# Two transformer blocks on one core: values of the dilated attention in token order, a merged projection block, another pace for the modulation, and expert weights in 8 KB tiles

## Chip, cores and metric

The kernel runs on one core of a Trainium2 chip. The metric is the device time of one execution in microseconds (us). A core has a tensor engine for products (PE, with its loads of the stationary operand, PEld), a vector engine (DVE), a scalar engine (ACT), GpSimd (POOL) and a sync engine (SP) that issues most of the transfers, in order.

## What is computed

A first block of two layers (gated linear attention, short convolution, neighbourhood attention, a convolutional FFN; 512 tokens, and a context of 256 in layer 0), then a second block with four branches over the same 512 tokens (A dilated window attention, B sparse attention with an index, C a time mix, D a state-space mixer), and a mixture of 32 experts, two per token. The parts that the change touches, cut from the reference:

```python
mod = jax.nn.silu(c) @ w_ada[layer] + b_ada[layer]                 # modulation: 6 vectors of 1024
u = modulate(rmsnorm(x, norm_mix_g[layer]), sh1, sc1) @ w_in[layer]
...
A_PATTERNS = ((128, 1), (512, 4), (2048, 16))                      # window, dilation
for q, kp, vp, (win, dil) in zip(qs, kps, vps, A_PATTERNS):
    qb = ...reshape(b, nq, dil, A_HEADS, HEAD_DIM)                 # tokens by residue class
    s = jnp.einsum('barhe,bcrhe->brhac', qb, kb).astype(jnp.float32) * scale
    ...
    o = jnp.einsum('brhac,bcrhe->barhe', p, vb)
...
expert = g_sel * EXPERTS_PER_GROUP + e_sel                         # 2 of 32 experts for each token
return grouped_expert_ffn(x2d, expert, gate, w_gate, w_up, w_down) # silu(x Wg) * (x Wu) @ Wd
```

## The kernel before

Activations lie transposed, channels on partitions and tokens along the rows. Most products keep float32 accuracy by splitting both operands into a high part (`whi`, `hi`; cast on ACT, L287) and a low part (`wlo`, `lo`; difference on DVE, L289): three products, high by high, low by high, high by low, make one (L829 in the first block, L191 to L195 and L1222 to L1224 in the second). Raw weights come by SP (L276) into a few tiles of `k.wpool`. A planner (`Weave.run`) interleaves generator streams: each `yield` names an engine and an estimated cost, and the planner issues the step that can start first; so the order on each engine is fixed when the program is built.

*First block.* `layer` makes one block of 128 output channels after another: `blk` loads a block of `w_in_t`, and `dense` does eight rounds of three products on 512 latent and, where wanted, 256 context columns. Heads 4 and 5 of the gated linear attention are 64 channels in k and in q; each of the two blocks GK45 and GQ45 holds its 64 channels twice, so that both partition halves have them. Between blocks `more(n)` works off n pieces of a queue, `k.adaq` (L255 to L260): "H" pieces load 512 KB of `w_adaH` and take four products on DVE, "B" turns a finished vector round, "P" and "F" are pieces for PE. n is `ada_n`, 0.6 in layer 0 and 0.4 in layer 1. A norm that needs a modulation vector makes all pieces that are still missing (`need`).

*Second block.* `second` lists the streams. `dense2` makes one block of 128 channels of a branch, `values2` the values with tokens on partitions: for each of 4 chunks of 128 tokens and 8 of 128 channels, three products whose stationary operand is the token slice of x (`x2h`, `x2l`) and whose moving operand is 256 columns of weights. `StageA.values` (L1833) does this for the three dilations; group 0 takes adjacent tokens (`nat`), groups 1 and 2 every fourth token (`res`), since `StageA.attend` works on one residue class r at a time. `stage_vb` does the same for branch B (`k.vb`). Results of this size lie in the pool `t1`, 16 tiles of 1 KB per partition: 4 hold `vb` until the last B attend, 12 the three groups' values, and masks and probabilities use what is left. `t2` has 34 tiles of 2 KB. `StageB.index` finds the 256 largest scores by 16 rounds on DVE.

*Experts.* `experts` computes 33 blocks of 64 token rows: experts 0 to 22 in order, a second block for a busy expert at place 23 (after place 22), then the others; `expert_block` takes 16 products for gate and up and 8 for down. Weights of an expert are six parts of 1 MB. Experts with even numbers are loaded into 24 `t2` tiles by 24 transfers of 256 KB (2 KB of each partition's row, L2328), those with odd numbers into six `ew` tiles by transfers of 1 MB (8 KB rows, L2323); there are seven `ew` tiles, in the pool `ep`, which lies over the space of weights, x2 and the branch weights. At the start of block p the loads of expert p + 2 are issued. Each block's output goes to DRAM (`yd`). `gates` computes the gate values on DVE ahead of block 0. `beyond` is a loop for further blocks; it does not run on these inputs (33 output copies for 33 blocks).

Of the kernel before, what the change touches and what calls it, by code (L numbers as in the profile page):

```python
# [239 lines left out]
def ada_prep(k):  # L240

    nc = k.nc
    cc = k.cpool.tile([128, 8, 2], FT, name="cc", tag="cc")
    nc.sync.dma_start(cc, k.ap["c2"])
    k.cs = k.cpool.tile([128, 8, 32], FT, name="cs", tag="cs")
    nc.gpsimd.memset(k.cs, 0.0)
    k.act(k.cs[:, :, 0:2], cc, AF.Silu)
    k.ada_due = 0
    k.mods, k.bada, k.g = {}, {}, {}
    tiles = lambda *qs: [4 * q + i for i in range(4) for q in qs]  # L250

# [586 lines left out]
GLR, GK0, GQ0, GK45, GQ45, NAK, NAQ, GR, SCC, SCH, SCB = 0, 1, 2, 3, 4, 5, 8, 11, 14, 16, 18  # L838


def layer(k, w, l, x, xt, src):
# [116 lines left out]
    ada_n = 0.6 if upd else 0.4  # L958
# [250 lines left out]
def values2(k, name, j, kcs, n, view, store):  # L1209
# [21 lines left out]
nat = lambda x, t: x[:, t * 128:(t + 1) * 128]  # L1231
res = lambda x, t: x[:, t::4]
# [351 lines left out]
def stage_vb(k):  # L1584
# [8 lines left out]
    yield from values2(k, "w2_vb", None, (4, 4), 264, nat, store)  # L1593
# [233 lines left out]
class StageA:  # L1827
# [489 lines left out]
def load_expert(k, src, small):  # L2317

    out = [None] * 24
    for j in (0, 2, 1, 3, 4, 5):  # L2320
        w = None if small else k.ep.tile([128, 2048], FT, tag="ew", name="ew", bufs=k.NEW)
# [7 lines left out]
    return out  # L2329


def rows(k, blks, blk):
# [4 lines left out]
    oh = [t1(k, [128, 4 // n, n, 64]) for _ in range(n)]  # L2337
# [10 lines left out]
    def part(i, after=None):  # L2348
# [9 lines left out]
        out.append(t1(k, [128, 2, 64 * n]))  # L2358
# [5 lines left out]
def expert_block(k, x, W, ydst, queue, fill=()):  # L2364
# [15 lines left out]
    HT = t1(k, [128, 4, 64])  # L2380
# [14 lines left out]
def experts(k, W, routing):  # L2395
# [24 lines left out]
    gates(k)  # L2420
    for i, b in enumerate(order):
        p = b if b < 32 else SWAP
        if 0 < p < 30 and b < 32:
            W.append(load(p + 2))
        if b == 31:
            n = nc.values_load(k.eid[0:1, 16:17], min_val=0, max_val=15)
        if b == 30:
            ln2 = [[t2(k) for _ in range(2)] for _ in range(2)]
            for a in range(2):
                for h in range(2):  # L2430
                    nc.sync.dma_start(ln2[a][h], k.ap["ln2"][a][:, h * 512:(h + 1) * 512])
# [9 lines left out]
def beyond(k, n):  # L2441

    tc, nc = k.tc, k.nc
    with tc.For_i(0, n, 1) as i:  # L2444
# [5 lines left out]

        def weights(n):
            t = k.ep.tile([128, 512], FT, tag="bw", name="bw", bufs=4)
            nc.sync.dma_start(t, k.ap["w_exp"][bass.ds(e, 1), n // 4].rearrange("a p n -> (a p) n")[:, n % 4 * 512:n % 4 * 512 + 512])
            return t
# [7 lines left out]
def gates(k):  # L2462
# [5 lines left out]
    for t in range(4):  # L2468
        d = t1(k, [128, 2, 128])
# [5 lines left out]
def finish(k, ln2, out):  # L2475
# [9 lines left out]
    for t in range(4):  # L2485
        y = k.ep.tile([128, 2048], FT, tag="ew", name="ew", bufs=k.NEW)
# [130 lines left out]
def body(tc, ap):  # L2617
    nc = tc.nc
    with ExitStack() as st:
# [4 lines left out]
        k.csd = k.dp.tile([2, 128, 1024], FT, name="csd", tag="csd")  # L2624
        k.yd = k.dp.tile([NB * 64, 1024], FT, name="yd", tag="yd")
# [3 lines left out]
        with ExitStack() as sw:  # L2629
            k.wpool = sw.enter_context(tc.tile_pool(name="w", bufs=1, side="right"))  # L2630
            with ExitStack() as s1:
# [25 lines left out]
                k.hp = sw.enter_context(tc.tile_pool(name="h2", bufs=1, side="right"))  # L2657
# [12 lines left out]
        next(routing)  # L2670
        finish(k, experts(k, W, routing), ap["out"])
# [6 lines left out]
def hostprep(I):  # L2678
# [17 lines left out]
    cols=[w[:,:,768:800],z, w[:,:,192:320], w[:,:,0:128], w[:,:,320:384],w[:,:,320:384], w[:,:,128:192],w[:,:,128:192], w[:,:,2336:2720], w[:,:,1952:2336], w[:,:,800:1184], w[:,:,1440:1696], w[:,:,1696:1952], w[:,:,1184:1440]]  # L2696
# [133 lines left out]
```

## Time and profile before

| | us |
|---|---|
| median of three executions | 3198.53 (3196.09 to 3203.12) |
| the profiled execution | 3198.1 |
| its span | 3196.2 |
| PE busy | 3003.7 (94%) |
| PE's stationary loads busy | 2275.4 (71%) |
| DVE busy | 1531.5 (48%) |
| ACT busy | 989.5 (31%) |
| POOL busy | 565.8 (18%) |

The first block runs to about 1830, the second to about 2648, the experts to 3163, then the sum of two outputs per token and the last norm. The rows below come from one profiled execution. In a timeline a row is one instruction, or xN alike ones in a row, with its start and length; PE's matmuls overlap, so what a matmul costs is the distance between starts and not its length. "PEld" is the load of the stationary operand. In the table of stretches the granted clock is a share of PE's full clock, and the DMA share is the mean busy share of the core's 16 DMA engines. A row of waits names the engine, tile and line that waited, and what ended the wait.

### The profile page before, as it was taken

How to read it: one execution, taken by the hardware profiler on the slowest of the kernel's cores; microseconds unless marked ns; L12 is line 12 of the kernel's file. 1: busy time of each engine (PE TensorE's matmuls, PEld its weight loads, DVE VectorE, ACT ScalarE, POOL GpSimd, SP SyncE). 2: the span in 40 equal slices, each digit the busy share in tenths (PEclk: the TensorE clock that was granted, in tenths of full speed). 3: DMA queues.
4: the chain of work that ended last, by engine and by line, in shares of the span. 5: the costliest groups of instructions: out<-in, count | busy, mean ns of one | idle time of the engine just before them, and what ended most of it. 6: DMA issues, size and time to landing. Idle time of an engine off the chain costs nothing. (4 is left out here: it accounts for less than half of the span.)

```text
span 3196.2 us, 42551 instructions
## 1 busy us (share of the span) xinstructions
PE 3003.7 (94%) x16248; PEld 2275.4 (71%) x16248; DVE 1531.5 (48%) x3049; ACT 989.5 (31%) x1649; POOL 565.8 (18%) x569
## 2 busy tenths in 40 slices
PE   7999997999999899989999999999998989999998
PEld 5878676888887687767777778878776765544453
DVE  3566857644536626744443456525545562111112
ACT  4243314322323324343332443233242521111111
POOL 2331301210102123131121131220001010000002
PEclk9999998999999899999999999999998999999999
DMA  6411333322324431232222330042131359999997
GB/s 232 142 57 49 120 107 98 107 85 86 109 83 148 132 94 58 69 99 79 90 93 89 96 109 21 14 142 73 55 106 47 98 196 352 393 378 389 391 396 290
DMA packets 159838, 461.29 MB, mean 144 GB/s; under 512 B 20912, under 2 KB 28752, under 8 KB 147344
## 3 DMA queue, kind: packets, MB, share of 16 engines
q1 hardware_dynamic: 145296, 434.05, 38.7%
q0 software_dynamic: 7776, 19.70, 1.8%
q10 hardware_dynamic: 6560, 4.79, 0.5%
q8 instruction: 130, 2.13, 0.3%
q14 instruction: 76, 0.62, 0.1%
HBM read 435.40 MB, written 19.92 MB: 142 GB/s over the span
## 5 line engine op out<-in xcount | busy, mean ns | idle before, releaser
L289 DVE TENSOR_TENSOR wlo<-wraw,whi 128x1024 fp32r<-128x1024 f32 (+2 forms) x276 | 339.4, 1231 | 444.9 <-ACT whi L287 427.9
L287 ACT CAST whi<-wraw 128x1024 fp32r<-128x1024 f32 (+2 forms) x276 | 285.6, 1036 | 793.6 <-PE at L829 287.7
L829 PE MATMUL mm<-hi,whi 128*128 128x512 f32 (+1 forms) x1152 | 476.1, 416 | 33.1 <-ACT hi L448 13.8
L829 PE MATMUL mm<-lo,whi 128*128 128x512 f32 (+1 forms) x1152 | 462.2, 401 | 11.9 <-DVE lo L451 10.8
L829 PE MATMUL mm<-hi,wlo 128*128 128x512 f32 (+1 forms) x1152 | 458.9, 400 | 14.6 <-DVE wlo L289 14.5
L829 PEld LDWEIGHTS mm<-hi,whi 128*128 128x128 f32 (+1 forms) x1152 | 217.1, 189 | 106.7 <-issue 32.9
L829 PEld LDWEIGHTS mm<-hi,wlo 128*128 128x128 f32 (+1 forms) x1152 | 217.6, 189 | 72.2 <-DVE wlo L289 17.4
L829 PEld LDWEIGHTS mm<-lo,whi 128*128 128x128 f32 (+1 forms) x1152 | 217.6, 189 | 64.0 <-DVE lo L451 12.2
L829 PE MATMUL mm<-b,whi 128*128 128x512 f32 x704 | 242.9, 398 | 7.1 <-ACT whi L287 6.5
L191 PE MATMUL mm<-x2h,whi 128*128 128x512 f32 x512 | 210.9, 413 | 7.3 <-ACT pcx L1251 4.7
L195 PE MATMUL mm<-x2h,wlo 128*128 128x512 f32 x512 | 204.3, 399 | 2.0 <-DVE wlo L289 2.0
L193 PE MATMUL mm<-x2l,whi 128*128 128x512 f32 x512 | 205.1, 401 | 0.1
L1120 POOL TENSOR_TENSOR b<-b,b 128x768 f32<-128x768 f32 (+1 forms) x44 | 71.9, 1635 | 679.4 <-DVE b L797 650.5
L2374 DVE COPY GU<-mm 64x512 f32<-64x512 f32 x33 | 22.9, 694 | 352.8 <-ACT GU L171 352.8
L829 PEld LDWEIGHTS mm<-b,whi 128*128 128x128 f32 x704 | 132.2, 189 | 40.8 <-ACT whi L287 7.8
L2354 PEld LDWEIGHTS gl<-t,gt 128*128 128x128 f32 x1088 | 128.0, 194 | 30.1 <-issue 16.4
L1087 DVE SCALAR_TENSOR_TENSOR b<-mm,mods,b 128x512 f32<-128x512 f32 x64 | 48.0, 750 | 210.3 <-PE mm L829 210.3
L2354 PE MATMUL gl<-t,gt 128*128 128x128 f32 (+1 forms) x1088 | 136.8, 280 | 3.8 <-DVE t L2344 3.8
L829 PE MATMUL mm<-b,wlo 128*128 128x512 f32 x352 | 138.6, 398 | 1.3 <-DVE wlo L289 1.2
L2371 PE MATMUL mm<-ew,t 128*64 128x512 f32 x256 | 117.7, 609 | 16.4 <-DMA ew<-w_exp 16.3
L829 PE MATMUL at<-hi,whi 128*128 128x256 f32 x416 | 118.2, 284 | 2.1 <-ACT hi L448 2.0
L191 PEld LDWEIGHTS mm<-x2h,whi 128*128 128x128 f32 x512 | 97.9, 191 | 31.3 <-ACT pcx L1251 5.1
(570 smaller groups left out, 6488.5 us busy)
## 6 DMA issues: line engine op xcount, KB each, us to landing
t<-w_exp SPq DMA_DIRECT2D x384, 256.0 KB, 5.9
ew<-w_exp SPq DMA_DIRECT2D x96, 1024.0 KB, 12.2
wraw<-ffn_up SPq DMA_DIRECT2D x88, 512.0 KB, 3.3
wraw<-w_t SPq DMA_DIRECT2D x64, 512.0 KB, 3.3
wraw<-w_adaH SPq DMA_DIRECT2D x48, 512.0 KB, 3.3
wraw<-w_in_t SPq DMA_DIRECT2D x40, 512.0 KB, 3.5
wraw<-w_adaF SPq DMA_DIRECT2D x32, 512.0 KB, 3.6
wraw<-ffn_dn SPq DMA_DIRECT2D x32, 448.0 KB, 3.2
```

The source lines that it names most:

```text
L191: nc.tensor.matmul(ps, whi[:, i, :], xs_(xh, kc, ts), start=st, stop=False)
L193: nc.tensor.matmul(ps, whi[:, i, :], xs_(xl, kc, ts), start=False, stop=False)
L195: nc.tensor.matmul(ps, wlo[:, i, :], xs_(xh, kc, ts), start=False, stop=sp)
L287: nc.scalar.copy(hi, raw)
L289: nc.vector.tensor_tensor(lo, raw, hi.bitcast(FT), op=OP.subtract)
L829: nc.tensor.matmul(p, w[:, kc - min(kcs)], x[:, sl], start=a, stop=e)
L1087: nc.vector.scalar_tensor_tensor(x[m][:, sl], p, k.mods[l][:, 8 * q + m, s:s + 1], x[m][:, sl], op0=OP.mult, op1=OP.add)
L1120: nc.gpsimd.tensor_tensor(y0[:, :N], y0[:, :N], y1[:, :N], op=OP.mult)
L2354: mm = nc.tensor.matmul(ps[:, c], k.x1[t][h][:, cs], oh[t * n // 4][:, t % (4 // n)].rearrange("p a b -> p (a b)"), start=(t == 0), stop=( ...
L2371: last = nc.tensor.matmul(gu[64:128], x(kc), W(8 + kc), start=(kc == 0), stop=(kc == 7)).ins
L2374: nc.vector.tensor_copy(GU[64:128], gu[64:128])
```

## The change

- `StageA.values`: groups 1 and 2 also take adjacent tokens. Each chunk's result is written to a DRAM buffer `vd` (128 KB), and four loads with row step 4 bring the residue classes into four new `t1` tiles.
- `layer`: GK45 and GQ45 become one block GKQ (64 channels of k, 64 of q); its evacuation `twice` writes each half to both partition halves by copies. `w_in_t` has 19 blocks per layer instead of 20.
- Modulation: `ada_n` is 1.05 in layer 0 and 0.7 in layer 1; the queue goes vector by vector, with five turns instead of four.
- Experts: all but expert 0 are loaded in parts of 1 MB into 19 tiles of 8 KB rows, `ew` (7) and `ew2` (12). `ew2` is opened after block 0, when the pools of constants `c3` and of `t1`, `t2` (`b2`) are closed; the rest of expert 2 is loaded and the gates are computed then. Rows, gathered inputs and HT are in a new tag `s1` (14 tiles). At the start expert 1's first five parts are loaded, then expert 0, expert 1's last part and expert 2's first.
- Pools: the first block's weight pool `w` closes behind it; the second block has its own, `w2`, beside `h2` on the right side.

The core of the diff (the weights' layout on the host, the output norm's tiles and the loop `beyond` are left out):

```diff
-    a, b, c = tiles(2), tiles(3, 4) + tiles(5), tiles(0, 1)
-    k.adaq += H(0, a, 1, True) + [("B", 0)] + H(0, a, 0, False) + H(0, b, 0, True) + [("B", 1)] + H(0, b, 1, False)
-    k.adaq += H(1, c, 1, True) + [("B", 0)] + H(1, c, 0, False) + [("B", 2)]
+    h = 1
+    for l, js in ((0, tiles(2)), (0, tiles(3, 4)), (0, tiles(5)), (1, tiles(0, 1))):
+        k.adaq += H(l, js, h, True) + [("B", 1 - h)] + H(l, js, 1 - h, False)
+        h = 1 - h
+    k.adaq.append(("B", 2))
...
-GLR, GK0, GQ0, GK45, GQ45, NAK, NAQ, GR, SCC, SCH, SCB = 0, 1, 2, 3, 4, 5, 8, 11, 14, 16, 18
+GLR, GK0, GQ0, GKQ, NAK, NAQ, GR, SCC, SCH, SCB = 0, 1, 2, 3, 4, 7, 10, 13, 15, 17
...
-    ada_n = 0.6 if upd else 0.4
+    ada_n = 1.05 if upd else 0.7
...
+    def twice(ps):
+
+        for d, p, c in ((g.kk, 0, True), (g.q, 64, upd)):
+            t = d[1] = k.b3()
+            yield cA(1.1)
+            for h in (0, 64):
+                nc.scalar.copy(t[h:h + 64, LAT], ps[0][p:p + 64])
+            if c:
+                yield cV(0.6)
+                for h in (0, 64):
+                    nc.vector.tensor_copy(t[h:h + 64, CTX], ps[1][p:p + 64])
+
     tk, tq = [None] * 2, [None] * 2
-    for i in range(2):
-        tk[i] = blk(GK0 + 2 * i, True, to(g.kk, i, True))
-        more(ada_n)
-        tq[i] = blk(GQ0 + 2 * i, upd, to(g.q, i, upd))
-        more(ada_n)
+    tk[0] = blk(GK0, True, to(g.kk, 0, True))
+    more(ada_n)
+    tq[0] = blk(GQ0, upd, to(g.q, 0, upd))
+    more(ada_n)
+    tk[1] = tq[1] = blk(GKQ, True, twice)
+    more(2 * ada_n)
...
-            h, l = view(xh[:, kc], t), view(xl[:, kc], t)
+            h, l = (x[:, kc, t * 128:(t + 1) * 128] for x in (xh, xl))
...
     def values(s, g):
         k, nc = s.k, s.k.nc
         v = s.v[g] = [t1(k) for _ in range(4)]
-        yield from values2(k, "w2_va", g, (4, 4), 256, nat if g == 0 else res, lambda t, ps: nc.scalar.copy(v[t], ps))
+        if g == 0:
+            yield from values2(k, "w2_va", g, (4, 4), 256, lambda t, ps: nc.scalar.copy(v[t], ps))
+            return
+
+
+        def store(t, ps):
+            nc.scalar.copy(v[t], ps)
+            nc.sync.dma_start(k.vd[g - 1, t * 128:(t + 1) * 128], v[t])
+        yield from values2(k, "w2_va", g, (4, 4), 256, store)
+        s.v[g] = [t1(k) for _ in range(4)]
+        yield cN(2.5)
+        for r in range(4):
+            nc.sync.dma_start(s.v[g][r], k.vd[g - 1, r::4])
...
-def load_expert(k, src, small):
-
-    out = [None] * 24
-    for j in (0, 2, 1, 3, 4, 5):
-        w = None if small else k.ep.tile([128, 2048], FT, tag="ew", name="ew", bufs=k.NEW)
+def big(k):
+
+    k.turns = (k.turns + 1) % (k.NEW + k.NEW2) if k.ep2 else (k.turns + 1) % k.NEW
+    if k.turns < k.NEW:
+        return k.ep.tile([128, 2048], FT, tag="ew", name="ew", bufs=k.NEW)
+    return k.ep2.tile([128, 2048], FT, tag="ew2", name="ew2", bufs=k.NEW2)
+
+
+def s1(k, shape):
+    return k.ep.tile(list(shape), FT, tag="s1", name="s1", bufs=k.NS1)
+
+
+def load_parts(k, out, js, src, small=False):
+
+    for j in js:
+        w = None if small else big(k)
         if w:
             k.nc.sync.dma_start(w, src(j, slice(0, 2048)))
         for c in range(4):
@@ -2326,7 +2360,9 @@
             out[4 * j + c] = t2(k) if small else w[:, cs]
             if small:
                 k.nc.sync.dma_start(out[4 * j + c], src(j, cs))
-    return out
+
+
+PARTS = (0, 2, 1, 3, 4, 5)
...
-    oh = [t1(k, [128, 4 // n, n, 64]) for _ in range(n)]
+    oh = [s1(k, [128, 4 // n, n, 64]) for _ in range(n)]
...
     def load(p):
-        small = p % 2 == 0
+        W.append([None] * 24)
         if p < EARLY:
-            return load_expert(k, lambda j, c: k.ap["w_exp"][p, j][:, c], small)
+            load_parts(k, W[p], PARTS, lambda j, c: k.ap["w_exp"][p, j][:, c])
+            return
         e = nc.values_load(k.eid[0:1, 17 + p:18 + p], engines=(mybir.EngineType.SP,), min_val=0, max_val=31)
-        return load_expert(k, lambda j, c: k.ap["w_exp"][bass.ds(e, 1), j].rearrange("a p n -> (a p) n")[:, c], small)
-
-    W.append(load(2))
+        load_parts(k, W[p], PARTS, lambda j, c: k.ap["w_exp"][bass.ds(e, 1), j].rearrange("a p n -> (a p) n")[:, c])
+
     for f in gather(0, k.blk0):
         f()
     drain(routing)
-    gates(k)
...
-            W.append(load(p + 2))
+            load(p + 2)
...
+        if i == 0:
+            sb.close()
+            k.ep2 = k.pool("ep2")
+            load_parts(k, W[2], PARTS[k.NEW - 6:], lambda j, c: k.ap["w_exp"][2, j][:, c])
+            gates(k)
...
+                s0.close()
+                k.hp = right(sw, "h2")
+                k.wpool = right(sw, "w2")
...
-            k.c2, k.gtp, k.b2p = k.pool("c2"), k.pool("gt"), k.pool("b2")
-            k.brp = sw.enter_context(tc.tile_pool(name="br", bufs=1, side="right"))
-            k.NT2, k.NT1, k.NEW = 34, 16, 7
-            consts2(k)
-            acc = [t2(k) for _ in range(8)]
-            second(k, acc)
-            W = [load_expert(k, lambda j, c: ap["w_exp"][0, j][:, c], True)]
-        k.ep = k.pool("ep")
-        W.append(load_expert(k, lambda j, c: ap["w_exp"][1, j][:, c], False))
+        k.c2, k.gtp = k.pool("c2"), k.pool("gt")
+        k.c3, k.b2p = (sb.enter_context(tc.tile_pool(name=n, bufs=1)) for n in ("c3", "b2"))
+        k.brp = right(sw, "br")
+        k.NT2, k.NT1, k.NEW, k.NEW2, k.NS1, k.turns, k.ep2 = 34, 16, 7, 12, 14, -1, None
+        consts2(k)
+        acc = [t2(k) for _ in range(8)]
+        second(k, acc)
+        sw.close()
+        k.ep = right(st, "ep")
+        W = [[None] * 24 for _ in range(3)]
+        for p, js in ((1, PARTS[:5]), (0, PARTS), (1, PARTS[5:]), (2, PARTS[:k.NEW - 6])):
+            load_parts(k, W[p], js, lambda j, c, p=p: ap["w_exp"][p, j][:, c], p == 0)
```

## Rows read from the trace of the kernel before

**Rows 1.** Stretches: us; busy us (count) PE, PEld, DVE, ACT, POOL; clock, DMA share, GB/s.
```profile
2648.40:2810.00 161.60, 161.60 (x927) 82.06 (x928) 31.05 (x113) 20.59 (x44) 10.44 (x20) 1.00 0.99 373
2810.00:2997.00 187.00, 173.31 (x926) 84.74 (x924) 25.72 (x81) 21.11 (x44) 11.37 (x22) 0.98 1.01 387
2997.00:3163.00 166.00, 160.15 (x894) 79.32 (x890) 19.99 (x51) 20.71 (x44) 10.33 (x20) 1.00 0.99 382
```
**Rows 2.** Stretches of the second block's middle (columns as in rows 1).
```profile
2171.00:2220.00 49.00, 47.59 (x208) 40.49 (x207) 25.63 (x45) 15.39 (x32) 2.88 (x2) 1.00 0.17 54
2220.00:2280.00 60.00, 53.97 (x226) 42.28 (x225) 54.22 (x114) 17.56 (x25) 7.73 (x6) 0.94 0.21 71
```
**Rows 3.** Waits of PE, 2655 to 3163.
```profile
PE mm L2371 <- DMA ew<-w_exp: 16.3, 11, 2.1
```
**Rows 4.** Groups by line, stationary loads, 2155 to 2171; busy us, mean ns | idle before.
```profile
L1222 PEld LDWEIGHTS mm<-whi,x2h 128*128 128x128 f32 x32 | 6.1, 189 | 0.3
```
**Rows 5.** Groups by line, stationary loads, 2280 to 2307.
```profile
L1222 PEld LDWEIGHTS mm<-whi,x2h 128*128 128x128 f32 x31 | 10.2, 328 | 0.3 <-issue 0.2
```
**Rows 6.** Timeline of PE at 2159: start us, us, line, operation.
```profile
2158.92 0.28 PE L1224 MATMUL mm<-whi,x2l 128*128 128x256 f32 x1
...
2159.27 0.28 PE L1224 MATMUL mm<-whi,x2l 128*128 128x256 f32 x1
```
**Rows 7.** Timeline of PE at 2297.
```profile
2297.14 0.40 PE L1224 MATMUL mm<-whi,x2l 128*128 128x256 f32 x1
...
2297.84 0.40 PE L1224 MATMUL mm<-whi,x2l 128*128 128x256 f32 x1
```
**Rows 8.** The tile Y: an expert block's output copies and their write-backs.
```profile
L2390 ACT COPY Y<-mc x33: 586/586/587, 2663.4 to 3162.8; 128x512 f32<-128x512 f32 x33
...
DMA to landing us min/median/max: 2.3/4.3/7.3
```
**Rows 9.** Timeline of PE at 373, layer 0's projections.
```profile
373.11 0.40 PE L829 MATMUL mm<-hi,whi 128*128 128x512 f32 x1
...
375.22 0.39 PE L829 MATMUL mm<-hi,whi 128*128 128x512 f32 x1
```
**Rows 10.** Timeline of PE at 1310, layer 1's projections.
```profile
1309.60 0.39 PE L829 MATMUL mm<-hi,whi 128*128 128x512 f32 x1
...
1311.69 0.40 PE L829 MATMUL mm<-hi,whi 128*128 128x512 f32 x1
```
**Rows 11.** Timeline of SP's load queue, 290 to 520 (consecutive issues in one row).
```profile
359.19 24.96 SPq L276 DMA_DIRECT2D wraw<-w_adaH  x8
```
**Rows 12.** Waits of PE, 380 to 510: total us, times, longest us.
```profile
PE mm L829 <- DVE wlo L289: 13.6, 2, 8.4
```
**Rows 13.** Stretches of the expert loads (columns as in rows 1).
```profile
2908.00:2914.00 6.00, 6.00 (x27) 2.02 (x28) 0.42 (x1) 0.59 (x1) 1.03 (x2) 1.00 1.02 427
...
2956.00:2968.00 12.00, 12.00 (x70) 5.88 (x71) 2.46 (x11) 1.33 (x3) 1.03 (x2) 1.00 1.05 388
2834.90:2852.90 18.00, 14.40 (x71) 5.68 (x70) 0.85 (x2) 1.52 (x4) 1.03 (x2) 1.00 1.02 418
2810.00:3120.00 310.00, 296.31 (x1620) 146.41 (x1618) 41.78 (x124) 37.08 (x77) 20.67 (x40) 0.99 1.02 389
```
**Rows 14.** Timeline of SP's load queue, 2570 to 2680.
```profile
2577.47 43.84 SPq L2328 DMA_DIRECT2D t<-w_exp  x24
2622.67 3.61 SPq L2323 DMA_DIRECT2D ew<-w_exp  x6
```
**Rows 15.** Timeline of SP's load queue, 1790 to 1870.
```profile
1805.36 20.19 SPq L276 DMA_DIRECT2D wraw<-w_t  x5
```
**Rows 16.** Timeline of PE, 1821 to 1831.
```profile
1822.50 0.40 PE L829 MATMUL mm<-b,wlo 128*128 128x512 f32 x1
...
1830.34 1.19 PE L191 MATMUL mm<-x2h,whi 128*128 128x512 f32 x2 [0.48 <-ACT x2h L205]
```
**Rows 17.** Timeline of PE, 2440 to 2447, the last attend of the sparse branch.
```profile
2444.12 1.11 PE L1994 MATMUL mc<-t,t 128*64 128x128 f32 x6 [0.46 <-ACT t L1986]
```

More of the change, by code (lines that the diff above doesn't have):

```diff
@@ L1154, in ld @@
 def ld(k, name, shape, dt=FT, key=None):
-    t = k.c2.tile(shape, dt, name=name, tag=name)
+    t = (k.c3 if name in ("tri", "trig", "caus", "pm", "lev", "bd64", "lora") else k.c2).tile(shape, dt, name=name, tag=name)
     k.nc.sync.dma_start(t, k.ap[name])
@@ L1206, in dense2, with values2 @@
     yield "-", "mm", 1
-def values2(k, name, j, kcs, n, view, store):
+def values2(k, name, j, kcs, n, store):
     nc = k.nc
@@ L1228, in values2 @@
     yield "-", "s", 2
-nat = lambda x, t: x[:, t * 128:(t + 1) * 128]
-res = lambda x, t: x[:, t::4]
 class StageC:
@@ L1592, in store @@
         nc.vector.tensor_copy(k.ex[:, t], ps[:, 256:264])
-    yield from values2(k, "w2_vb", None, (4, 4), 264, nat, store)
+    yield from values2(k, "w2_vb", None, (4, 4), 264, store)
 class StageD:
@@ L2357, in part @@
                     k.order(after, mm)
-        out.append(t1(k, [128, 2, 64 * n]))
+        out.append(s1(k, [128, 2, 64 * n]))
         (nc.vector.tensor_copy if i % 2 else nc.scalar.copy)(out[-1], ps)
@@ L2379, in expert_block @@
         last = nc.tensor.transpose(ht[:, i], GU[:, i * 128:(i + 1) * 128], k.c["ident"]).ins
-    HT = t1(k, [128, 4, 64])
+    HT = s1(k, [128, 4, 64])
     nc.scalar.copy(HT, ht[:, :, 0:64])
@@ L2392, in expert_block, with experts @@
         queue.dma_start(ydst[:, h * 512:(h + 1) * 512], Y[h * 64:(h + 1) * 64])
-def experts(k, W, routing):
+def experts(k, W, routing, sb):
     nc = k.nc
@@ L2427, in experts @@
         if b == 30:
-            ln2 = [[t2(k) for _ in range(2)] for _ in range(2)]
+            t = big(k)
+            ln2 = [[t[:, (2 * a + h) * 512:(2 * a + h + 1) * 512] for h in range(2)] for a in range(2)]
             for a in range(2):
-                for h in range(2):
-                    nc.sync.dma_start(ln2[a][h], k.ap["ln2"][a][:, h * 512:(h + 1) * 512])
+                nc.sync.dma_start(t[:, a * 1024:(a + 1) * 1024], k.ap["ln2"][a])
         if i % 2 == 0:
@@ L2449, in beyond @@
         e = nc.values_load(ec, min_val=0, max_val=31)
+        w = [None] * 6
         def weights(n):
-            t = k.ep.tile([128, 512], FT, tag="bw", name="bw", bufs=4)
-            nc.sync.dma_start(t, k.ap["w_exp"][bass.ds(e, 1), n // 4].rearrange("a p n -> (a p) n")[:, n % 4 * 512:n % 4 * 512 + 512])
-            return t
+            if w[n // 4] is None:
+                w[n // 4] = k.ep.tile([128, 2048], FT, tag="ew", name="ew", bufs=k.NEW)
+                nc.sync.dma_start(w[n // 4], k.ap["w_exp"][bass.ds(e, 1), n // 4].rearrange("a p n -> (a p) n"))
+            return w[n // 4][:, n % 4 * 512:n % 4 * 512 + 512]
         t, parts = rows(k, [bc], k.blk)
@@ L2468, in gates @@
     for t in range(4):
-        d = t1(k, [128, 2, 128])
+        d = k.ep2.tile([128, 2, 128], FT, tag="dg", name="dg", bufs=4)
         for j in range(2):
@@ L2485, in finish @@
     for t in range(4):
-        y = k.ep.tile([128, 2048], FT, tag="ew", name="ew", bufs=k.NEW)
+        y = big(k)
         ys.append((y[:, 0:1024], y[:, 1024:2048]))
@@ L2624, in body @@
         k.csd = k.dp.tile([2, 128, 1024], FT, name="csd", tag="csd")
+        k.vd = k.dp.tile([2, 512, 256], FT, name="vd", tag="vd")
         k.yd = k.dp.tile([NB * 64, 1024], FT, name="yd", tag="yd")
@@ L2628, in body @@
         consts(k)
-        with ExitStack() as sw:
-            k.wpool = sw.enter_context(tc.tile_pool(name="w", bufs=1, side="right"))
-            with ExitStack() as s1:
+        right = lambda st, name: st.enter_context(tc.tile_pool(name=name, bufs=1, side="right"))
+        sw = ExitStack()
+        sb = ExitStack()
+        with ExitStack() as s1:
+            if True:
+                s0 = ExitStack()
+                k.wpool = right(s0, "w")
                 o, k.st = k.st, s1
@@ L2656, in body @@
                 sh.close()
-                k.hp = sw.enter_context(tc.tile_pool(name="h2", bufs=1, side="right"))
+                s0.close()
+                k.hp = right(sw, "h2")
+                k.wpool = right(sw, "w2")
                 k.x2 = tuple(k.hp.tile([128, 8, 512], FR, tag=n, name=n) for n in ("x2h", "x2l"))
                 final_norm(k, x)
-            k.c2, k.gtp, k.b2p = k.pool("c2"), k.pool("gt"), k.pool("b2")
-            k.brp = sw.enter_context(tc.tile_pool(name="br", bufs=1, side="right"))
-            k.NT2, k.NT1, k.NEW = 34, 16, 7
-            consts2(k)
-            acc = [t2(k) for _ in range(8)]
-            second(k, acc)
-            W = [load_expert(k, lambda j, c: ap["w_exp"][0, j][:, c], True)]
-        k.ep = k.pool("ep")
-        W.append(load_expert(k, lambda j, c: ap["w_exp"][1, j][:, c], False))
+        k.c2, k.gtp = k.pool("c2"), k.pool("gt")
[10 more added lines that the diff above has]
+            load_parts(k, W[p], js, lambda j, c, p=p: ap["w_exp"][p, j][:, c], p == 0)
         routing = router(k)
         next(routing)
-        finish(k, experts(k, W, routing), ap["out"])
+        finish(k, experts(k, W, routing, sb), ap["out"])
 def f32(a):
@@ L2695, in hostprep @@
     z=np.zeros((2,1024,96),np.float32)
-    cols=[w[:,:,768:800],z, w[:,:,192:320], w[:,:,0:128], w[:,:,320:384],w[:,:,320:384], w[:,:,128:192],w[:,:,128:192], w[:,:,2336:2720], w[:,:,1952:2336], w[:,:,800:1184], w[:,:,1440:1696], w[:,:,1696:1952], w[:,:,1184:1440]]
+    cols=[w[:,:,768:800],z, w[:,:,192:320], w[:,:,0:128], w[:,:,320:384], w[:,:,128:192], w[:,:,2336:2720], w[:,:,1952:2336], w[:,:,800:1184], w[:,:,1440:1696], w[:,:,1696:1952], w[:,:,1184:1440]]
     o['w_in_t']=blkT(np.concatenate(cols,-1))
```

## The prediction

> **What bounds the kernel now.** I first cut the span into stages by their lines and read the table by stage, then the waits of PE in each stage, then the matmuls one by one for their price, and for the expert stage the load queue and the transfer rates. TensorE sets the time almost everywhere: eleven expert blocks are 161.6 us busy out of 161.6, while the two stretches behind them idle for 13.7 and 5.8 us [rows 1]. So an edit that removes PE time is worth its full issue distance, unless a chain on another engine runs beside it; in the second block there is one such place, where VectorE is busy 54.2 of 60 us [rows 2]. Late in the expert stage the transfers take over: the DMA share there is 1.01 and 0.99, at 387 and 382 GB/s [rows 1]. PE's chief named wait there is for expert weights, 16.3 us in 11 waits [rows 3].
>
> The sum is made against the profiled execution, 3198.1 us (span 3196.2 and 1.9 around it), which is 0.4 below the median of the three times, 3198.53.
>
> **Values in token order.** `StageA.values` for groups 1 and 2 loads as stationary operand a slice of every fourth token. A load takes 189 ns where tokens are adjacent [rows 4] and 328 ns where they are four apart [rows 5]. That exceeds the 256-column matmul beside it, so it sets the pace: three matmuls follow each other in 2159.27 − 2158.92 = 0.35 us, 0.117 each [rows 6], against 2297.84 − 2297.14 = 0.70, 0.233 each [rows 7]. Two groups by 4 chunks by 8 by 3 are 192 matmuls; 192 × 0.116 = 22.3 us. The change adds 8 stores and 8 loads of 128 KB on SP. Both sit in the in-order queue, with later weight loads behind them. The store must land before the load may go: the write-backs of the experts' outputs land after 2.3 to 7.3 us [rows 8], so SP is held some 5 to 10 us per group. Weights prefetched ahead hide that, and if the cover is gone it costs up to 2 × 7.3 = 15. I charge 1: **−21** (bounds −22 and −6).
>
> The Trainium skill speaks against this part. "TensorE: Matmul & The Clock Gate", section "LDWEIGHTS (loading the stationary operand)", has the time of a load depend on its columns alone, P / 1.2 ns, and P is 128 in either layout: by that rule the part would gain nothing and the kernel would end at 3160. The trace disagrees, 189 ns against 328 for the same 128 columns.
>
> **One block for k and q of heads 4, 5.** Two duplicated blocks of 128 columns become one; 8 × 3 = 24 products fall away per layer. In layer 0 each is a pair (512 latent and 256 context columns): six pairs start between 373.11 and 375.22, 0.352 us each [rows 9]; 24 × 0.352 = 8.4. Layer 1 has the context only in k, so what goes is q's block of 512 columns: nine start between 1309.60 and 1311.69, 0.232 each [rows 10]; 24 × 0.232 = 5.6. One weight load and split per layer go too, off the path. Added are 4 ACT and 2 to 4 DVE copies of 64 rows per layer, beside PE's next block. **−14**; bounds −14 and −9, if PE waited for all eight ACT copies at the 0.59 us of a 512-column copy [rows 8].
>
> **Modulation pace.** The queue of weight pieces (`adaq`) is used at 0.6 per call, 17 such units in the in-projection and 8 in `w_out` of layer 0: 17 × 0.6 + 8 × 0.6 = 15 pieces. The norm ahead of layer 0's FFN needs 28, so the rest come in bursts: eight w_adaH loads in a row from 359.19 on SP, a run of 25 us [rows 11], each piece with its products on DVE ahead of the split of the next weights. Between 380 and 510 PE waits 13.6 us for the low part of split weights, which DVE makes [rows 12]. At 1.05 the same units give 17.85 + 8.4 = 26 pieces, and in the new order the norm needs 24. So the burst at the norm should go, and what is late next is the norm's own chain. Not all of the 13.6 is the burst's: the first weights of a stage may be waited for anyway, and denser pieces take DVE time in the in-projection. I take half, **−7**; bounds 0 (the waits only move) and −13.6.
>
> **Experts.** A block takes 161.6 / 11 = 14.7 us of PE [rows 1]; the 22 further blocks from 2810 to 3163 take 353 us for 22 × 14.7 = 323, so 30 us are waits. An expert is 6.29 MB and a block writes back 0.26, together 6.55. At the 389 of the whole late stretch [rows 13] that is 16.8 us per expert. Stretches with 8 KB rows alone move 427 GB/s, with 2 KB rows alone 388, and one of 1 MB loads with the write-backs 418 [rows 13]. With all experts in 8 KB rows I take 418 to 427: 15.3 to 15.7, say 15.6, still 0.9 over a block. The lead changes also. Before, expert loads run nearly without a break from 2577.47 [rows 14]. The `ew` tiles come free at 2622.67 [rows 14]; after, they take the rest of experts 0 and 1 and one part of expert 2, at least 7.3 MB, on chip by about 2642. The 12 `ew2` tiles lie over buffers that block 0 uses, so from there nothing can be loaded until block 0's last product, whose output copy starts at 2663.4 [rows 8]. Then five parts of expert 2 and all of expert 3 (11.5 MB, some 27 us with latency) land near 2692, with block 3 due at 2648.4 + 3 × 14.7 = 2692.5; its last gate part is first read some 5 us into the block and lands 5 us before the expert is complete, so about 7.5 us of slack are left there. Up to the repeated block at place 22 the loads fall behind by 19 × 0.9 = 17; 17 − 7.5 = 10 us of waits, then the repeated block gives 14.7 back. **−20** (30 to 10). At 15.3 us it is −25; at the old 16.8, 19 × 2.1 − 7.5 = 32 of waits and **+2**. Expert 1's loads now stand ahead of expert 0's in the program: if expert 0 had to follow 5.2 MB of them from 2622.67, block 0 would wait some 5 us more; I count it in the range only.
>
> **Pools.** The second block's weight buffers move to a new pool that lies over the old block's. Five w_t loads ran from 1805.36 [rows 15]; now they wait for the last product of the first block, at 1822.50 [rows 16]. The first product of the second block starts at 1830.34 [rows 16], which leaves 7.8 us for landing, cast and split. A landing takes 2.3 to 7.3 us (the write-backs' row again [rows 8]), so the cost is 0 where all fits, and twice the longest landing less the 7.8, 6.8, where cast and split and the constants' loads take as long again. **+2.5** (0 to 6.8). The gates moved behind block 0 run on DVE, which is busy 31 of 161.6 us there [rows 1]: nothing.
>
> Sum: −21 − 14 − 7 − 20 + 2.5 = −59.5; 3198.1 − 59.5 = **3138.6**, I say 3139.
>
> **Rivals.**
> *Index chain.* In 2220 to 2280 DVE is nearly full and PE is not [rows 2]; if this chain, not PE, sets when the B and A attends end, the matmuls saved before it turn into waits and only those behind it count: half of the values, 3149, or none, 3160. Against it: PE is busy 47.6 of 49 us just before [rows 2]. Chance 0.13.
> *Transfer rate.* If the rate is set by the memory and not by the row length, or if the pause until block 0 ends costs the lead that I count, the experts gain nothing: 3198.1 − 21 − 14 − 7 + 2 + 2.5 = 3161. For it: only short stretches are free of the other kind. Against it: 427 and 388 side by side [rows 13]. Chance 0.13. The Trainium skill's "DMA: Bandwidth & Descriptors", "Where 436 GB/s comes from", holds that about 358 GB/s of memory bandwidth per core bind for such loads; by that rule tile size would be worth nothing and this rival's time would follow. The trace disagrees, at 387 over 187 us and 427 at best.
> *The stride is not the cause* of the slower loads (it is some neighbour's port use): nothing from values, 3160. Chance 0.04.
> *Slower: the small-tile pool.* Sixteen `t1` tiles hold vb (4) and v (12); with natural-order tiles group 2 fills all sixteen until its stores land. If a load of v gets a slot that vb holds until the last B attend, whose products run at 2444.12 [rows 17], SP stands from about 2298 [rows 7] with the weights behind it, up to 146 us: 3198.1 − 59.5 + 146 = 3285. It decides from a wait of 60 us beyond the weights already on chip. Against it: the natural tiles come free first. Chance 0.05.
> *Everything hidden better:* pace at its −13, experts without waits (−30): 3123 or a little less. Chance 0.09.
>
> **How the numbers follow.** The forecast's own case (3128 to 3148) has 0.56; index chain 0.13, rate 0.13, stride 0.04, better 0.09, slower 0.05. The range 3115 to 3168 takes in all but the slow one and combinations of two bad cases. The three times lie within 7 us, so 0.2% (6.4 us) is about what can be told from no change: faster 0.92, same 0.03, slower 0.05.
>
> **What would show it.** Stationary loads of `values2` near 190 ns throughout; one block less in each in-projection; no row of eight w_adaH loads ahead of the FFN of layer 0; DMA near 420 GB/s from 2700 on, weight waits under 15 us and the first of them later than block 11; a first product of the second block some 2 us later behind the last of the first. Wrong would be: strided-like loads on natural slices, SP standing behind a regrouping load, PE waiting longer on DVE around the index, or a DMA rate still under 400.

## The result, and the profile after

The changed kernel takes 3161.06 us (median of 3155.86 to 3162.91) against 3198.81 for the kernel before: ratio 0.9878, 95% interval 0.9861 to 0.9895. That is 37.8 us less; 59.5 were forecast. The profiled execution, 3155.86 us with a span of 3154.1, is the quickest of the four. So sizes are taken below from the medians, and from stage lengths that several traces share, and not from this one span.

Values: the groups of stationary loads between 2120 and 2300 (busy us, mean ns | idle before).

```profile
L1237 PEld LDWEIGHTS mm<-whi,x2h 128*128 128x128 f32 x96 | 18.1, 190 | 1.8 <-ACT whi L289 0.9 <-issue 0.4
L1238 PEld LDWEIGHTS mm<-wlo,x2h 128*128 128x128 f32 x96 | 18.1, 189 | 0.8 <-issue 0.2
L1239 PEld LDWEIGHTS mm<-whi,x2l 128*128 128x128 f32 x96 | 18.0, 189 | 0.9 <-issue 0.8
```

All 288 loads of the three groups now take 189 to 190 ns; two thirds of them took about 330 before ([rows 4, 5]).

Experts: the table of stretches (us; busy us and count of PE, PEld, DVE, ACT, POOL; granted clock, DMA share, GB/s), then the row of the tile Y, then the waits for expert weights between 2630 and 3125 of PE's matmuls and of its stationary loads.

```profile
2784.00:2971.00 187.00, 186.12 (x999) 91.45 (x996) 26.41 (x82) 22.32 (x46) 12.41 (x24) 1.00 1.01 420
2700.00:3100.00 400.00, 399.12 (x2220) 200.95 (x2216) 57.49 (x170) 50.73 (x106) 26.87 (x52) 1.00 1.01 420
```

```profile
L2426 ACT COPY Y<-mc x33: 586/586/587, 2637.5 to 3120.7; 128x512 f32<-128x512 f32 x33
```

```profile
PE mm L2407 <- DMA ew<-w_exp: 0.7, 1, 0.7
...
PEld mm L2407 <- DMA ew<-w_exp: 10.8, 14, 1.6
```

The transfers now run at 420 GB/s where 387 and 389 stood ([rows 1, 13]). From the first to the last output copy the stage takes 483.2 us, against 3162.8 − 2663.4 = 499.4 before ([rows 8]). PE's named wait for weights is gone (16.3 in [rows 3]), but the DMA share is still 1.01: the copies of blocks 8 to 22 come about 15.6 us apart, those ahead of block 8 at 14.7. What still holds PE shows at its loads of the stationary operand: 10.8 us in 14 waits, where the kernel before had 33.9 us in 25.

The modulation pieces ahead of `w_out` of layer 0, on SP's load queue:

```profile
339.33 9.88 SPq L278 DMA_DIRECT2D wraw<-w_adaH  x2
...
357.66 19.85 SPq L278 DMA_DIRECT2D wraw<-w_adaH  x7
...
383.16 0.33 SPq L278 DMA_DIRECT2D wraw<-w_adaH  x1
```

The run of eight pieces that stood at 359.19 ([rows 11]) stands there still, as seven from 357.66.

To see where the 37.8 us are, I set stage against stage in the traces. Each number of this table is the distance between two starts: that of the first matmul of one norm's statistics (L417, L419 in the changed kernel) and that of the next. The experiments' rows stand here too; they are told below. "Pace" is the queue order and the rate `ada_n` together.

| us | first norm to FFN norm, layer 0 | FFN of layer 0 | mixers of layer 1 | FFN of layer 1 |
|---|---|---|---|---|
| before | 457.6 | 605.8 | 345.9 | 397.1 |
| the change | 457.0 | 600.6 | 347.3 | 399.8 |
| merge alone | 448.1 | 605.0 | 340.7 | 398.8 |
| pace alone | 467.8 | 602.6 | 349.3 | 396.7 |
| the change, old pace | 447.2 | 603.6 | 341.1 | 395.5 |
| the change, new order at the old rate | 437.1 | 607.6 | 344.2 | 395.8 |
| the change, no products of H pieces | 428.7 | 583.2 | 346.8 | 398.0 |
| the change, own buffer for pieces | 465.6 | 578.6 | 339.4 | 394.4 |
| the change, faster beside `w_out` only | 440.2 | 605.0 | 345.9 | 397.0 |
| the change, four shared buffers | 459.5 | 603.5 | 340.3 | 394.3 |

In the first block the change gains 0.6 + 5.2 − 1.4 − 2.7 = 1.7 us in all. Forecast were 21, 14 for the merge and 7 for the pace. So the question for the chip was which of the two didn't come.

### The profile page after: what moved, and what is told of

Its sections match the earlier page's. It is cut to its first block, busy times and chain, and to the rows that moved or that the text cites. A ratio compares the mean times of both kernels' runs of the same rounds, so it can differ in the third digit from the quotient of the medians.

```text
span 3154.1 us, 41559 instructions
## 1 busy us (share of the span) xinstructions
PE 2973.0 (94%) x16176; PEld 2242.6 (71%) x16176; DVE 1537.9 (49%) x3050; ACT 990.9 (31%) x1653; POOL 568.7 (18%) x569
## 5 line engine op out<-in xcount | busy, mean ns | idle before, releaser
L291 DVE TENSOR_TENSOR wlo<-wraw,whi 128x1024 fp32r<-128x1024 f32 (+1 forms) x274 | 334.9, 1223 | 459.9 <-ACT whi L289 442.4
L289 ACT CAST whi<-wraw 128x1024 fp32r<-128x1024 f32 (+1 forms) x274 | 283.5, 1036 | 806.7 <-PE at L831 303.8
L831 PE MATMUL mm<-lo,whi 128*128 128x512 f32 (+1 forms) x1136 | 457.8, 403 | 13.8 <-DVE lo L453 13.4
L831 PEld LDWEIGHTS mm<-hi,wlo 128*128 128x128 f32 (+1 forms) x1136 | 215.8, 190 | 63.5 <-DVE wlo L291 10.8
L2407 PE MATMUL mm<-ew,s 128*64 128x512 f32 x512 | 227.8, 594 | 0.9 <-DMA ew<-w_exp 0.7
L2406 PE MATMUL mm<-ew,s 128*64 128x512 f32 x512 | 226.1, 593 | 0.0
L2406 PEld LDWEIGHTS mm<-ew,s 128*64 128x64 f32 x512 | 69.1, 137 | 121.3 <-issue 120.6
L2390 PEld LDWEIGHTS gl<-s,gt 128*128 128x128 f32 x1088 | 128.1, 194 | 29.4 <-issue 20.3
L2390 PE MATMUL gl<-s,gt 128*128 128x128 f32 (+1 forms) x1088 | 136.8, 280 | 3.3 <-DVE s L2380 3.3
```

The lines of the kernel that those rows point to most:

```text
L289: nc.scalar.copy(hi, raw)
L291: nc.vector.tensor_tensor(lo, raw, hi.bitcast(FT), op=OP.subtract)
L831: nc.tensor.matmul(p, w[:, kc - min(kcs)], x[:, sl], start=a, stop=e)
L2390: mm = nc.tensor.matmul(ps[:, c], k.x1[t][h][:, cs], oh[t * n // 4][:, t % (4 // n)].rearrange("p a b -> p (a b)"), start=(t == 0), stop=( ...
L2406: nc.tensor.matmul(gu[0:64], x(kc), W(kc), start=(kc == 0), stop=(kc == 7))
L2407: last = nc.tensor.matmul(gu[64:128], x(kc), W(8 + kc), start=(kc == 0), stop=(kc == 7)).ins
```

## Experiments

**Merge alone**, in the kernel before:

```diff
-GLR, GK0, GQ0, GK45, GQ45, NAK, ... = 0, 1, 2, 3, 4, 5, ...
+GLR, GK0, GQ0, GKQ, NAK, ... = 0, 1, 2, 3, 4, ...
+    tk[1] = tq[1] = blk(GKQ, True, twice)
```

> The kernel before with the merged block of heads 4 and 5 alone. Prediction's step (PE-bound projections): 14 us faster, about 3184. Theory now (the gated attention's chain and the w_out weights set the end of both mixers, so PE time saved before them turns into waits): 0 to 5 us faster, 3194 to 3198, with layer 0 some 8 us ahead until about 340 and the lead gone at the norm ahead of the FFN.

Measured: 3185.77 us, ratio 0.9956 (0.994 to 0.9972), 14.7 less. My theory after the result (that the attention's chain eats the gain) fell, and the prediction's step stood. The starts of the norms ahead of the two FFN parts (timeline of PE, the norms' statistics; the first two rows are the FFN norm and the next first norm in the kernel before, the other two those of the merge alone):

```profile
475.38 1.45 PE L417 MATMUL at<-b,ones 128*128 128x512 f32 x4
1081.20 1.56 PE L417 MATMUL at<-b,ones 128*128 128x512 f32 x4 [1.24 <-POOL b L408]
```

```profile
465.08 1.45 PE L417 MATMUL at<-b,ones 128*128 128x512 f32 x4
...
1070.11 1.56 PE L417 MATMUL at<-b,ones 128*128 128x512 f32 x4 [1.01 <-POOL b L408]
```

Layer 0 is 9.5 us shorter up to its FFN norm and layer 1's mixers 5.2 (the table); 8.4 and 5.6 were counted.

**Pace alone**, in the kernel before: the new queue order, and

```diff
-    ada_n = 0.6 if upd else 0.4
+    ada_n = 1.05 if upd else 0.7
```

> The kernel before with the new order and pace of the modulation pieces alone. Prediction's step: 7 us faster, about 3191. Theory now (the burst at the norm goes, worth 8 to 12 us there, but the same products on VectorE come back as a cluster beside the FFN of layer 0 and at the end of layer 1's mixers): 0 to 4 us faster, 3194 to 3198, with PE's lead at 650 about 10 us and at 870 only 2. Rival (the loss in the FFN belongs to the merge): 8 to 11 faster.

Measured: 3212.53 us, ratio 1.0041 (1.0027 to 1.0055): 12 us slower, which none of the three expectations had. PE's matmuls, set against the same matmuls before in their order, are 0.5 us ahead at 98 and 7.7 behind at 189, 10.6 behind at the norm, 1.3 ahead just behind it, and 11 behind at 870. So a gain at the norm is there, 11.9 us, and two losses stand against it. Stretches of the kernel before first, then the same work with the new pace:

```profile
98.00:189.00 91.00, 89.10 (x527) 70.81 (x526) 51.87 (x125) 27.56 (x54) 26.33 (x31) 1.00 0.32 103
755.00:870.00 115.00, 114.05 (x647) 99.03 (x646) 67.32 (x119) 39.85 (x53) 23.32 (x12) 1.00 0.33 109
```

```profile
97.50:196.70 99.20, 91.58 (x527) 72.32 (x526) 72.54 (x181) 27.64 (x54) 27.58 (x31) 0.98 0.41 133
755.00:881.00 126.00, 118.32 (x649) 101.78 (x648) 80.75 (x146) 40.22 (x54) 28.76 (x14) 0.97 0.31 103
```

And PE's longest waits on DVE with the new pace, in the first stretch and in the second; then that of the kernel before in the second:

```profile
PE mc L831 <- DVE b L897: 4.1, 1, 4.1
```

```profile
PE mm L831 <- DVE b L799: 6.8, 4, 2.2
```

```profile
PE mm L829 <- DVE b L797: 0.8, 1, 0.8
```

The same 527 matmuls take 8.2 us longer beside 20.7 us more of VectorE work; PE waits there for an evacuation on DVE (L897). In the FFN of layer 0 some 648 matmuls take 11 longer beside 13.4 more; PE waits there for convolution steps on DVE (L799, L797 before) that free its PSUM tiles.

**Values alone**, in the kernel before:

```diff
-            h, l = view(xh[:, kc], t), view(xl[:, kc], t)
+            h, l = (x[:, kc, t * 128:(t + 1) * 128] for x in (xh, xl))
...
+            nc.sync.dma_start(k.vd[g - 1, t * 128:(t + 1) * 128], v[t])
...
+            nc.sync.dma_start(s.v[g][r], k.vd[g - 1, r::4])
```

> The kernel before with the values in token order alone. Theory (the strided stationary load sets the pace, and nothing else takes its place): 18 to 21 us faster, 3177 to 3180. Rival (index chain on VectorE): 11 or less. Rival (small-tile pool): slower.

Measured: 3179.24 us, ratio 0.9928 (0.9911 to 0.9944), 21.2 less. Predicted −21. The index chain and the small-tile pool don't show: counted back from PE's last matmul, the work from the 5600th to the 4800th and from there to the 3100th, with the two groups in it, takes 150.5 + 359.7 us here, 155.3 + 377.0 before, and 152.7 + 359.8 in the changed kernel.

**2 KB rows into the same tiles**, in the changed kernel:

```diff
-            k.nc.sync.dma_start(w, src(j, slice(0, 2048)))
...
+            k.nc.sync.dma_start(out[4 * j + c], src(j, cs))   # c = 0..3, 512 columns each
```

> The changed kernel with the same 19 tiles, each filled by four loads of 512 columns (2 KB rows) instead of one of 2048. Theory (row length sets the rate): transfer rate of the expert stage falls from 420 to about 390 GB/s, an expert takes 16.8 instead of 15.6 us, and the stage is 15 to 22 us longer: 3176 to 3183. Rival (more buffers or the memory, not the row length): within 5 us of 3161.

Measured: 3219.98 us, 59 more than the changed kernel and 20 more than the kernel before (ratio to it 1.0055, 1.0034 to 1.0075). The direction is that of the row length, the size three times what I expected. Stretch 2700 to 3100, with 2 KB rows:

```profile
2700.00:3100.00 400.00, 372.28 (x1962) 182.00 (x1958) 51.98 (x159) 44.22 (x92) 24.81 (x48) 0.98 1.03 370
```

2 KB rows alone hold 370 GB/s over 400 us, and not the 388 that I had read from 12 us of the kernel before ([rows 13]). Those 12 us were a good moment: of six such stretches of the kernel before in which no 8 KB packet starts, they are the best, and these two the worst:

```profile
2820.00:2832.00 12.00, 12.00 (x66) 5.62 (x66) 2.32 (x10) 1.31 (x3) 1.03 (x2) 1.00 0.98 330
2856.00:2868.00 12.00, 12.00 (x60) 5.34 (x59) 1.90 (x10) 1.18 (x2) 1.03 (x2) 1.00 0.97 324
```

Of before's mixture, half and half, 389 is near the mean that 370 and 420 give (1 / (0.5 / 370 + 0.5 / 420) = 393). The edit makes each load a quarter as large (256 KB) as well as its rows; no run here separates the two.

**13 tiles instead of 19**, in the changed kernel:

```diff
-    k.NT2, k.NT1, k.NEW, k.NEW2, ... = 34, 16, 7, 12, ...
+    k.NT2, k.NT1, k.NEW, k.NEW2, ... = 34, 16, 7, 6, ...
```

> The changed kernel with 6 ew2 tiles instead of 12: 13 tiles of 1 MB, about the capacity of the kernel before (7 tiles and 6 MB in small tiles), still in 8 KB rows. Theory (row length sets the rate, capacity only the lead): rate stays at 415 to 420 GB/s, 0 to 10 us slower than the changed kernel. Rival (capacity is what the new tiles bring): 20 us slower or more, with the rate below 400.

Measured: 3157.74 us (ratio to before 0.9873, 0.985 to 0.9897), no slower than with 19. The rate is the same:

```profile
2700.00:3100.00 400.00, 399.22 (x2211) 199.41 (x2208) 56.80 (x169) 50.12 (x105) 27.16 (x53) 1.00 1.01 421
```

So the gain in the expert stage comes with the 1 MB loads of 8 KB rows and not with the number of tiles: six of them bring nothing that can be measured.

**The old pace in the changed kernel** (old order, 0.6 and 0.4):

> The changed kernel with the old queue order and the old pace of the modulation pieces (0.6 and 0.4). Theory (the pace costs 12 us wherever it is, and the merge then keeps its 14): 10 to 14 us faster than the changed kernel, 3146 to 3151. Rival (the pace helps beside the merge, as predicted at 7): 3166 to 3170. Rival (the merge's gain is lost in the changed kernel for another reason): about 3161.

Measured: 3143.92 us, ratio to before 0.9834 (0.9811 to 0.9856), 17 less than the changed kernel, more than the 10 to 14 expected. The merge's gain is back (447.2 and 341.1 in the table). Of the 17 us, the table has 9.8 up to the FFN norm, −3.0 in the FFN of layer 0, and 10.5 in layer 1.

**New order, old rate**, in the changed kernel (`ada_n` 0.6 and 0.4):

> The changed kernel with the new order of the queue, but the old rate (0.6 and 0.4). If the rate costs and the order doesn't: 9 us gained back in the in-projection, the norm's burst smaller than before (fewer pieces are needed ahead of it), 3140 to 3150. If the order is what moves pieces into the FFN of layer 0: 3155 to 3165.

Measured: 3141.39 us, ratio 0.9825 (0.9801 to 0.9849). Only the rate differs from the change, so the rate costs the 20 us between them: 457.0 − 437.1 = 19.9 up to the FFN norm, −7 in the FFN of layer 0, and 7 in layer 1. The order alone, set against the old pace, gains 10 up to the norm (447.2 to 437.1) and loses 4 in the FFN of layer 0 and 3 in layer 1.

**No products of the H pieces**, in the changed kernel:

```diff
-                V.tensor_tensor_reduce(r if s else k.junk, r, k.bc[...], 1.0, ..., OP.mult, OP.add, o)
+                V.tensor_copy(o, k.bada[l][:, 2 * j + b:2 * j + b + 1])
```

> The changed kernel without the products of the modulation's H pieces: their loads, turns and waits stay, VectorE only copies the bias column (so both layers' modulation from these pieces lacks its product, and the routing may differ; read up to the first expert block). Theory (VectorE's time for the pieces is what delays the evacuations): the first expert block starts 18 to 30 us earlier, with no lead lost at 100 to 190 nor at 755 to 870. Rival (the loads and their buffers are what delays the weights): within 5 us of the changed kernel.

Measured: 3112.30 us, ratio 0.9732 (0.9702 to 0.9762). The output copy of the first expert block starts at 2596.9 instead of 2637.5, 40.6 earlier, more than the 18 to 30 expected. The FFN of layer 0 takes 583.2 instead of 600.6, with 253.73 us of DVE work in its 585 instead of 318.62 in 601:

```profile
445.00:1030.00 585.00, 569.76 (x3187) 493.04 (x3186) 253.73 (x364) 177.16 (x233) 98.07 (x53) 0.99 0.29 96
```

```profile
474.00:1075.00 601.00, 571.17 (x3177) 491.83 (x3177) 318.62 (x503) 177.47 (x233) 100.22 (x53) 0.98 0.29 97
```

The first row is without the products, the second that of the change. So the loads alone are not what costs. But a piece without products also gives its weight buffer back at once, so this run does not tell VectorE's time from the buffer; the runs after it try to.

**A raw buffer of its own for the pieces**, in the changed kernel (one activation tile less pays for the 4 KB):

```diff
-    raw, = yield from load_raw(k, [k.ap["w_adaH"][l, j, h] if kind == "H" else ...], 1024)
+    yield "+", "wa", 1
+    raw = k.wpool.tile([128, 1024], FT, tag="araw", name="araw", bufs=1)
+    nc.sync.dma_start(raw, k.ap["w_adaH"][l, j, h] if kind == "H" else ...)
```

> The changed kernel (new order, rate 1.05 and 0.7) with one raw buffer of 4 KB for the modulation pieces alone, so that they do not take turns with the dense weights (one tile of 3 KB less for activations pays for it). Theory (pieces come in clusters because they wait for a weight buffer; spread out, VectorE's products hide): no stretch of 100 us without a piece, 3125 to 3145. Rival (at this rate the pieces collide with the in-projection wherever their buffer is): the 9 us at 100 to 190 stay, 3150 to 3160.

Measured: 3130.57 us, ratio 0.9786 (0.977 to 0.9803): 30 less than the change, and the best complete kernel here. The same with the old rate:

> The same with one raw buffer of its own, new order and the old rate (0.6 and 0.4), to be set against 3141 of the new order at the old rate with shared buffers. Theory of the buffer: 3122 to 3138. Rival (the rate alone matters): 3139 to 3145.

Measured: 3133.37 us, ratio 0.9799 (0.9783 to 0.9815). With a buffer of their own the pieces no longer care about the rate; in both kernels all 48 are loaded between 44 and 481 us, at the same times within 2 us, about one each 9 us, ahead of the FFN. Up to the FFN norm that costs 8.6 us more than the change (465.6 against 457.0, with DVE busy 335.18 of 423 us), the FFN of layer 0 takes 22 less, and layer 1 takes 13 less. The FFN, then the stretch ahead of it:

```profile
483.00:1062.00 579.00, 564.88 (x3177) 488.44 (x3178) 270.47 (x395) 178.31 (x234) 100.25 (x53) 0.99 0.29 94
60.00:483.00 423.00, 399.00 (x2378) 318.83 (x2377) 335.18 (x820) 133.93 (x260) 113.69 (x121) 0.98 0.37 125
```

So they didn't spread as I had thought; they moved to where they cost less.

**Faster beside `w_out` only**, in the changed kernel with 0.6 elsewhere (`more(1.4)` behind each block of `w_out` of layer 0):

> The changed kernel with the new order, the old rate of 0.6 in the in-projection, and 1.4 for each block of w_out of layer 0; shared buffers. If what is left of the cost is the flush at the norm: 3133 to 3139. If it is the cluster in the FFN of layer 0 or the products themselves: 3140 to 3146, against 3141 at 0.6 throughout.

Measured: 3143.13 us, ratio 0.9828 (0.981 to 0.9846), no better than 3141. But the edit hardly moved the pieces: in this kernel as in that at 0.6 throughout, 24 are loaded by 453 us, eight of them from 422 on. So the flush at the norm is still there, and this run does not tell what it costs.

**Four raw buffers, shared**, in the changed kernel (the same space as the buffer of its own):

> The changed kernel (new order, rate 1.05 and 0.7) with four raw buffers in the first block, shared by dense weights and modulation pieces, in place of three; the same space as the buffer of its own. If it is the number of buffers that was short: 3127 to 3140, as with the buffer of its own (3131). If the pieces' place is what matters (beside the FFN of layer 0, where they delay the evacuations): 3148 to 3165, with the FFN of layer 0 still over 595 us from norm to norm.

Measured: 3150.33 us, ratio 0.9845 (0.9824 to 0.9867). A fourth buffer gains 11 of the 30 us, in layer 1's mixers (340.3) and its FFN; layer 0 loses some 5, and its FFN stays at 603.5. So there one more buffer does not help: the last ten of this kernel's 48 loads still come between 719 and 828. With a buffer of their own they come ahead of the FFN, and dense weights no longer share theirs with them. How much of the price in the FFN is VectorE's time at that place, and how much the buffers held meanwhile, these runs leave open.

## Why the prediction came out as it did

The time lay within the range and on the forecast side, 22 us above the likeliest value. One step broke its own bounds; that the total still lay in the range is owed to the range's width. Step by step, from medians:

| step | predicted | measured | from |
|---|---|---|---|
| values | −21 | −21 | values alone |
| merge | −14 | −15 | merge alone |
| pace | −7 | +12 alone, +17 in the change | pace alone; the change less old pace |
| experts | −20 | −18 | last part of the trace, below |
| pools | +2.5 | about −1 | stretch behind the last norm, below |

Their sum, −21 − 15 + 17 − 18 − 1 = −38, agrees with the measured 37.8. Experts and pools had no run of their own; their sizes are read from stages of the traces.

**Values, merge.** Both were priced by issue distance on a stretch that PE bounds, and both medians came to within a microsecond when they stood alone (their intervals are some 5 us either way). The rule of the Trainium skill's "TensorE: Matmul & The Clock Gate", section "LDWEIGHTS (loading the stationary operand)", by which a load depends on its columns alone, would have had the values gain nothing; the 21.2 us decide against it. The Trainium skill's "SBUF — State Buffer", section "Specifications (TRN2)", has what would explain the trace: cachelines of 16 bytes, and a penalty for each access that crosses to a new one; a step of four float32 does so every time. That agrees with 189 against 330 ns; no run here varied the step.

**Pace: the failed step.** "I take half, −7; bounds 0 and −13.6." The wait that it priced was there and went. In the kernel before 8.4 of the 13.6 us stand behind the norm:

```profile
PE mm L829 <- DVE wlo L289: 8.4, 1, 8.4
```

With the pace alone 0.8 of it is left, and 11.9 us are won back at the norm. The row that the step took for the burst, at 359.19, stayed. But the bound "0 (the waits only move)" excluded a loss without a reason. The sentence ahead of it, that denser pieces take DVE time in the in-projection, named the loss and gave it no price; and nothing asked where the pieces behind the norm would go. The trace before had the price of a piece: four products of about 0.9 us each. PE's waits on DVE in the two stretches were still small there, 0.6 and 0.8 us. Ahead of 190 us 16 pieces are loaded in the change where 9 were; with the pace alone that stretch cost 8 us of PE time. The last 16 pieces, loaded between 553 and 811 us before, come between 599 and 837, seven of them from 797 on, beside the convolutions of the FFN. The rate is not a pace in time: `more` places a piece in the planner's list, and from there it starts when a weight buffer is free for it.

More than half of the 17 us in the change are in layer 1, 6.2 in its mixers and 4.3 in its FFN. The "F" pieces are not work for PE, as I wrote above: each is a load of 512 KB (`w_adaF`) and one product of 1024 columns on DVE, 1.38 us on average in the mixers. Eight of their loads fall into these mixers in the change, from 1318 to 1340, and two at the old pace. With four buffers or with their own none does, and the mixers take 340.3 and 339.4.

The table's first stage hid this: alone, the pace loses 10.2 us there and the merge gains 9.5, so the change (457.0) looks as if the merge had done nothing, and the pace's gain at the norm falls into the next stage. My theory after the result was a reading of that one trace, and the merge alone refuted it.

**Experts.** The new rate was predicted (15.6 us an expert, and 15.6 measured between copies), and the waits of about 10 us are 14 (483.2 − 32 × 14.66): they set in at block 8, where the slack of 7.5 us had put them behind block 11. PE's last 3100 matmuls, from the output projection to the end, take 605.4, 609.0, 601.7 and 609.2 us in the four kernels with the old loads, 587.6 to 589.6 in the nine with 1 MB loads from expert 1 on: 18 us between the means. The transfer-rate rival (3161) has the very time that came, for another reason: with 2 KB rows the kernel would be at 3220. What I had wrong is the price of a 2 KB row, 370 GB/s and not 388; since the kernel before had it in half of its loads only, and the whole stretch's 389 was taken for that, it did not enter the sum. Nor does another misreading: the loads from 2577.47 ([rows 14]) do not run nearly without a break but at 145 GB/s, with pauses.

**Pools.** The weights did have to wait: the first w_t load goes out at 1821.17 instead of 1805.36 ([rows 15]), and the transposes behind the norm wait 1.4 us longer; the second block's first product comes 8.1 us behind the first block's last, against 7.8. But the constants are now loaded in two lots, seven small ones ahead of the next weights, and PE's wait for the first evacuation of the second block fell. In the kernel before and in the change, waits of PE between 1780 and 1880:

```profile
PE mm L191 <- ACT pcx L1251: 4.7, 1, 4.7
```

```profile
PE mm L191 <- ACT pcx L1262: 1.6, 1, 1.6
```

From the last norm over PE's next 600 instructions it is 121.5 to 124.1 us in the four kernels with the old pools and 118.2 to 122.5 in the ten with the new: no loss. Why that wait fell was not tried.

Of the rivals, the index chain, the one that blames something else than the stride, and the slower one with the small-tile pool did not occur. That the pace could cost was no rival of its own, and it was the one that counted.

## What to carry to other kernels

Work that is moved on an engine off the critical path has a price at its new place: count the time that it takes there and what on the critical engine waits for that engine in the same stretch, and give the bound a sign only with a reason. Where several edits share a stage, a trace of all of them together can show a gain of one and a loss of another as nothing; run each alone before a mechanism is named. Load in large pieces with long rows: here 1 MB loads of 8 KB per partition hold 420 GB/s, and the same bytes in loads of 256 KB with 2 KB rows 370.

## What the runs showed of the hardware

The modulation's product of 512 columns on VectorE takes 0.75 us, or up to 2.36. Of the 192 in the changed kernel 164 take under 0.85, with a mean of 0.748, and GpSimd was busy with tensor operations during 4% of their time; the 28 slower ones have a mean of 1.95, and GpSimd was busy during 79% of theirs. Each of the 28 ends 0.54 or 0.55 us after a GpSimd tensor operation has ended. One pair of rows, DVE's and then GpSimd's:

```profile
804.00 2.33 DVE L384 CUSTOM_DVE_ANT_0 wraw<-wraw,bc,mods 128x512 f32<-128x512 f32 x1
```

```profile
803.40 2.39 POOL L1140 TENSOR_TENSOR b<-b,b 128x768 fp32r<-128x768 f32 x1 [2.48 <-ACT b L1138]
```

The Trainium skill's "SBUF — State Buffer", section "Terms", has the two engines share a port pair of which one holds the whole for an instruction while the other waits; these rows agree. It is one reason why a piece costs more beside the FFN, whose activations GpSimd multiplies: from 700 to 870 us in the change 40 products take 40.2 us, from 60 to 190 us 61 take 48.9.
